# Two of the four sums of gate/up weights formed by accumulating transfers, and five whole pairs instead of six

## The chip, the cores and the metric

One core of a Trainium2 chip runs the whole program. The metric is device microseconds of one execution; a kernel's time is the median of its runs. The engines are TensorE (PE in the profile; its weight loads are PEld), VectorE (DVE), ScalarE (ACT), GpSimd (POOL) and SyncE (SP, which only issues transfers here).

## What is computed

A trunk of two decoder layers on 512 tokens of width 1024, in float32. Each layer has two feed-forward blocks (FFN) around a mixer; so there are four FFNs, numbered 0 to 3 here, and two mixers.

```python
def swiglu(x, w_gate, w_up, w_down):
    return (jax.nn.silu(x @ w_gate) * (x @ w_up)) @ w_down

for layer in range(DEPTH):                    # DEPTH = 2, D_FF = 2816
    h = h + 0.5 * swiglu(rms_norm(h, ffn_norm[layer, 0]), ...)
    mixed = mla_gla_mixer(...) if layer % 2 == 0 else nsa_mixer(...)
    h = h + mixed
    h = h + 0.5 * swiglu(rms_norm(h, ffn_norm[layer, 1]), ...)
return rms_norm(h, final_norm)
```

## The kernel before

Activations lie transposed in SBUF (128 channels x 512 tokens, 8 tiles of x). Every float32 operand is split into a high part (a copy to the format float32r on ScalarE, L150) and a low part (the difference, on VectorE, L151), and a product is three matmuls: high by high, low by high, high by low (`mm3`, L145 to L147). Weights come in raw tiles of 512 KB by SP's queue (`raw`, L91), of which there are three, used in turn for all weights; their high and low parts have three buffers too (`whi`, `wlo`; `shi`, `slo` for up weights and for sums).

An FFN has 22 blocks of 128 hidden channels. A block is a **pair**: its gate and its up product. Two forms of a pair exist:

- **Whole** (`whole`, L366): gate and up weights as they are, each 8 x 3 matmuls of 512 columns into a bank `ps_gu`. The first NP = 6 pairs of an FFN are whole. They take x without the normalising factor `rb`, which is known only after the first of them.
- **By seven products** (`gate_up_steps`, L310): the 2 x 2 blocks (gate, up by two halves of the 1024 input channels) and x in 2 x 2 blocks (two halves of channels, two of tokens) are multiplied in the scheme of Strassen and Winograd with seven products instead of eight. Each is 4 x 3 matmuls of 256 columns (`product`) into `ps_a` or `ps_b`. It needs four sums of weight blocks (`gate_up`, L117: VectorE, L130 to L133, into `sa` and `sb`, one buffer each) and seven forms of x (`ffn_forms`, a generator that is advanced by one step after each whole pair). The sums are split as any weight: into `shi`, `slo` and, for one block that is no sum, `uhi`, `ulo`.

The forms of x take the buffers of the x tiles that the whole pairs read (14 in all): three forms fit beside these tiles, the last four come when the last whole pair has read them. They are made in the last step of the generator, after which the first pair by products starts (L417, L418).

Between the pairs stand **units** (`unit`, L390): the down product of a group of four or five blocks for 128 output channels, into `ps_d`, added to x by VectorE (L397). The weights of pair j+1 are asked for at the start of the turn of pair j (L412), ahead of the whole pair j in the program.

The order of each engine's instructions is set when the program is built: a scheduler goes through the instructions by their place in the program as priority, gives out buffers and models the time; each engine then runs its fixed order and waits on semaphores. An instruction whose inputs and buffers are free early can stand far ahead of its place.

Of the kernel before, what the change touches and what calls it, by code (L numbers as in the profile page):

```python
# [12 lines left out]
F32 = mybir.dt.float32  # L13
R = mybir.dt.float32r
I32 = mybir.dt.int32
AF = mybir.ActivationFunctionType
ALU = mybir.AluOpType
PSUM = bass.MemoryType.PSUM

P = 128  # L20
# [6 lines left out]
NEG = -1e30  # L27
TINY = 1e-30
GROUPS = ((0, 4), (4, 9), (9, 14), (14, 18), (18, 22))
NP = 6  # L30
WARM = 11
H = T // 2
AHEAD = 400
# [7 lines left out]
class Core:  # L41
# [55 lines left out]
    def sparts(self):  # L97
        return (self.fw.tile([P, 1024], R, name=n, tag=n, bufs=3) for n in ("shi", "slo"))

    def sum_tile(self, tag):  # L100
        return self.fw.tile([P, 1024], F32, name=tag, tag=tag, bufs=1)

    def open_sums(self):

        self.fws = ExitStack()
        self.fw = self.fws.enter_context(self.pool("sums", side="right"))
# [10 lines left out]
    def gate_up(self, f, j):  # L117


        V, a = self.nc.vector, self.a  # L120
        w = T
        g = self.raw(a["wgu"][f, j, 0], 1024)
        gh, gl = self.wparts()
        self.split(g, gh, gl)
        u = self.raw(a["wgu"][f, j, 1], 1024)
        ah, al = self.sparts()
        bh, bl = self.sparts()
        uh, ul = (self.fw.tile([P, w], R, name=n, tag=n, bufs=1) for n in ("uhi", "ulo"))
        av, bv = (self.sum_tile(n) for n in ("sa", "sb"))
        V.tensor_add(av[:, :w], g[:, :w], u[:, :w])  # L130
        V.tensor_add(av[:, w:], u[:, :w], u[:, w:])
        V.tensor_add(bv[:, :w], av[:, w:], g[:, :w])
        V.tensor_add(bv[:, w:], bv[:, :w], g[:, w:])  # L133
        self.split(av, ah, al)
        self.split(bv, bh, bl)
        self.split(u[:, w:], uh, ul)
        h0, h1 = slice(0, w), slice(w, 2 * w)
        return [
            (gh[:, h0], gl[:, h0]), (gh[:, h1], gl[:, h1]), (ah[:, h0], al[:, h0]), (bh[:, h0], bl[:, h0]),
            (uh, ul), (ah[:, h1], al[:, h1]), (bh[:, h1], bl[:, h1]),  # L140
        ]

    def mm3(self, ps, lh, ll, rh, rl, start, stop, **k):
# [208 lines left out]
    def ffn_body(self, f, gi, hp, meanwhile, fp, out):  # L352
        nc, a = self.nc, self.a
        V, S = nc.vector, nc.scalar
        if out is not None:
            self.form("gap")
        xs, end = self.ffn_input(gi)
        self.rb = None
        hid, todo, w, forms = {}, [], {}, []

        def done(j, gt, ut):
            V.tensor_mul(ut, gt, ut)
            t = hid[j] = hp.tile([P, 2, T], R, name="hid", tag="hid", bufs=HID)
            self.split(ut, t[:, 0], t[:, 1])

        def whole(j):  # L366

            pt = []
            for s in range(2):
                with ExitStack() as st:  # L370
                    if f and 0 < 2 * j + s < 4:
                        for i in end:
                            st.enter_context(self.tc.issue_after(i.ins))
                    wh, wl = self.first or self.wload(a["wgu"][f, j, s], 1024, keep=self.sparts() if s else None)
                self.first = None
                ps = self.ps("ps_gu", "gu")
                for k in range(KC):
                    c = slice(k * P, (k + 1) * P)
                    self.mm3(ps, wh[:, c], wl[:, c], *xs[k], k == 0, k == KC - 1)
                pt.append(ps)  # L380
            if self.rb is None:
                self.rb = self.norm_stats(None if f else self.sumsq(self.x, fast=True))[1]
            ts = [hp.tile([P, T], F32, name=n, tag=n, bufs=2) for n in ("gt", "ut")]
            for s, t in enumerate(ts):
                V.tensor_mul(t, pt[s], self.rb)
                if s == 0:
                    S.activation(t, t, AF.Silu)
            done(j, *ts)

        def unit(g, c):  # L390
            j0, j1 = g
            wh, wl = self.wload(a["wd"][f, c, :, j0 * P : j1 * P], (j1 - j0) * P)
            ps = self.ps("ps_d", "d")
            for j in range(j0, j1):
                m = slice((j - j0) * P, (j - j0 + 1) * P)
                self.mm3(ps, wh[:, m], wl[:, m], hid[j][:, 0], hid[j][:, 1], j == j0, j == j1 - 1)
            V.scalar_tensor_tensor(out=self.x[c], in0=ps, scalar=0.5, in1=self.x[c], op0=ALU.mult, op1=ALU.add)  # L397

        def steps(j):
            return self.gate_up_steps(hp, w.pop(j), forms, lambda gt, ut: done(j, gt, ut))  # L400

        if f == 0:
            ps = self.ps("warm", "st")
            for _ in range(WARM):
                nc.tensor.matmul(ps[:, :P], self.ones, self.ones, start=True, stop=True)
        making = self.ffn_forms(gi, hp, forms)
        cur = None
        for j in range(JC):
            g = next(i for i, (j0, j1) in enumerate(GROUPS) if j0 <= j < j1)
            if j == GROUPS[g][0] and g > 0:  # L410
                todo += [(GROUPS[g - 1], c) for c in range(KC)]
            if NP <= j + 1 < JC:  # L412
                w[j + 1] = self.gate_up(f, j + 1)
            if j < NP:
                whole(j)
                next(making, None)
                if j == NP - 1:  # L417
                    cur = steps(NP)  # L418
                    next(cur)
            else:  # L420
                for n in range(5):
                    next(cur)
                nxt = None
                if j + 1 < JC:
                    nxt = steps(j + 1)
                    next(nxt)
                next(cur, None)
                cur = nxt
            if j == 3 and meanwhile:
                meanwhile(hp)  # L430
            left = GROUPS[g][1] - j
            for _ in range(-(-len(todo) // left)):
                unit(*todo.pop(0))
        if fp:
            self.ffn_end(f, GROUPS[-1][0], hid, fp, out)
            return
        for c in range(KC):
            unit(GROUPS[-1], c)
# [1064 lines left out]
```

## Time and profile before

| | us |
|---|---|
| three runs, median | 2015.86 |
| lowest and highest | 2014.3 and 2016.45 |
| the profiled execution, its own time | 2014.43 |
| span in its trace, first to last instruction | 2012.6 |
| FFN 0 to 3, body (from the end of the start on) | 308.7, 313.0, 306.0, 313.4 |
| mean granted TensorE clock, share of 2.4 GHz | 0.994 |

The page gives busy times by engine, and the chain of work that ended last, followed back from the last instruction. A matmul's time in the trace is from its start to its modelled end; neighbours overlap, so the step from start to start tells the rate, and the duration doesn't. In square brackets behind an instruction stands how long its engine was idle before it, and what ended that.

### The profile page before, as it was taken

The page shows a single profiled execution, that of the slowest core. Times are in us where ns is not written, and L with a number is a line of the kernel's source. Part 1 is how long each engine was busy: PE and PEld are TensorE (multiplying, and loading weights), DVE is VectorE, ACT ScalarE, POOL GpSimd, SP SyncE. Part 2 cuts the span into 40 slices and gives each one's busy share as a digit, 9 for nine tenths or more (in the row PEclk, how much of TensorE's full clock was granted, in tenths as well). Part 3 has the DMA queues.
Part 4 walks back from the last instruction along what each step waited for, and adds up shares of the span by engine and source line. Part 5 has one row for each costly group of instructions (what it writes and reads, how often), then busy time and mean ns, then how long its engine had stood idle before and what let it go on. Part 6 is the DMA issues. An engine that isn't in the chain of part 4 may idle for free.

```text
span 2012.6 us, 31406 instructions
## 1 busy us (share of the span) xinstructions
PE 1967.7 (98%) x11956; PEld 1736.2 (86%) x11956; DVE 1495.5 (74%) x2569; ACT 1020.2 (51%) x1848; POOL 212.0 (11%) x258
## 2 busy tenths in 40 slices
PE   8999999999999999999999999999899999999997
PEld 6899998898778899998789999888687878999997
DVE  7877775678888677776877777677899868777774
ACT  6444443565674444444544444445598754444443
POOL 0000000200340000001000000111365410000002
PEclk9999999999999999999999999999899999999999
DMA  5333332321323232332323233354400033232332
GB/s 175 93 95 100 113 97 67 109 74 43 87 66 116 89 101 90 106 104 86 124 82 102 96 103 99 89 155 135 117 1 1 27 118 96 86 103 96 102 96 68
DMA packets 71191, 186.41 MB, mean 93 GB/s; under 512 B 9856, under 2 KB 13056, under 8 KB 71040
## 3 DMA queue, kind: packets, MB, share of 16 engines
q1 hardware_dynamic: 70608, 183.36, 29.6%
q8 instruction: 94, 1.54, 0.3%
q10 hardware_dynamic: 432, 1.05, 0.2%
q14 instruction: 57, 0.47, 0.1%
HBM read 172.84 MB, written 2.10 MB: 87 GB/s over the span
## 4 chain that ended last, share of the span: by engine, by line
PE 88%; DVE 6%; ACT 2%; issue 1%; DMA 1%; SPq 0%; POOL 0%; DVEq 0%; POOLq 0%; ACTq 0%
PE ps_d L145 8%; PE ps_d L147 8%; PE ps_d L146 8%; PE ps_a L145 6%; PE ps_a L147 6%; PE ps_a L146 6%; PE ps_b L145 5%; PE ps_b L147 5%; PE ps_b L146 5%; PE ps_gu L145 4%; PE ps_gu L147 4%; PE ps_gu L146 4%; PE ps_p L145 3%; PE ps_p L147 3%; PE ps_p L146 3%
## 5 line engine op out<-in xcount | busy, mean ns | idle before, releaser
L150 ACT CAST whi<-raw 128x512 fp32r<-128x512 f32 (+3 forms) x317 | 257.7, 815 | 353.1 <-PE ps_d L146 119.7
L151 DVE TENSOR_TENSOR wlo<-raw,whi 128x512 fp32r<-128x512 f32 (+3 forms) x317 | 304.4, 962 | 92.0 <-ACT whi L150 90.8
L145 PE MATMUL ps_d<-hid,whi 128*128 128x512 f32 x672 | 265.2, 398 | 0.0
L147 PE MATMUL ps_d<-hid,wlo 128*128 128x512 f32 x672 | 264.5, 395 | 0.0
L146 PE MATMUL ps_d<-hid,whi 128*128 128x512 f32 x672 | 263.6, 393 | 0.0
L145 PE MATMUL ps_a<-bh,shi 128*128 128x256 f32 x768 | 217.0, 283 | 0.0
L146 PE MATMUL ps_a<-bl,shi 128*128 128x256 f32 x768 | 216.5, 282 | 0.0
L147 PE MATMUL ps_a<-bh,slo 128*128 128x256 f32 x768 | 216.0, 281 | 0.0
L215 POOL TENSOR_TENSOR ssq<-ssq,sq 128x512 f32<-128x512 f32 x30 | 46.0, 1534 | 1098.4 <-ACT sq L214 1098.4
L147 PEld LDWEIGHTS ps_d<-hid,wlo 128*128 128x128 f32 x672 | 126.1, 188 | 30.4 <-DVE wlo L151 0.7
L145 PEld LDWEIGHTS ps_d<-hid,whi 128*128 128x128 f32 x672 | 126.1, 188 | 25.8 <-ACT whi L150 1.0
L146 PEld LDWEIGHTS ps_d<-hid,whi 128*128 128x128 f32 x672 | 126.2, 188 | 25.0
L146 PEld LDWEIGHTS ps_a<-bl,shi 128*128 128x128 f32 x768 | 144.6, 188 | 1.2
L147 PEld LDWEIGHTS ps_a<-bh,slo 128*128 128x128 f32 x768 | 145.2, 189 | 0.0
L145 PEld LDWEIGHTS ps_a<-bh,shi 128*128 128x128 f32 x768 | 144.1, 188 | 1.2
L130 DVE TENSOR_TENSOR sa<-raw 128x512 f32<-128x512 f32 x64 | 44.2, 690 | 131.7 <-DMA raw<-wgu 131.7
L397 DVE SCALAR_TENSOR_TENSOR x<-ps_d,x 128x512 f32<-128x512 f32 x152 | 104.0, 686 | 42.3 <-PE ps_d L147 42.0
L587 POOL TENSOR_TENSOR pr<-pr,sums 128x128 f32<-128x128 f32 (+3 forms) x160 | 114.1, 746 | 101.3 <-DVE sums L1007 19.8
L150 ACT CAST uhi<-raw 128x512 fp32r<-128x512 f32 x64 | 39.7, 621 | 160.5 <-PE ps_b L146 111.3
L150 ACT CAST shi<-sa 128x1024 fp32r<-128x1024 f32 x64 | 67.3, 1051 | 76.8 <-PE ps_a L146 67.9
L151 DVE TENSOR_TENSOR slo<-sa,shi 128x1024 fp32r<-128x1024 f32 x64 | 78.3, 1223 | 28.5 <-ACT shi L150 28.4
L568 ACT ACTIVATE pr<-sm_s,sm_m 128x512 f32<-128x512 f32 (+3 forms) x160 | 89.7, 564 | 12.1 <-DVE sm_m L564 11.6
(450 smaller groups left out, 5576.9 us busy)
## 6 DMA issues: line engine op xcount, KB each, us to landing
raw<-wgu SPq DMA_DIRECT2D x175, 512.0 KB, 3.8
raw<-wd SPq DMA_DIRECT2D x96, 256.0 KB, 2.7
raw<-wd SPq DMA_DIRECT2D x64, 320.0 KB, 2.9
raw<-wo SPq DMA_DIRECT2D x32, 256.0 KB, 2.8
raw<-w1t SPq DMA_DIRECT2D x16, 512.0 KB, 3.6
raw<-w0v SPq DMA_DIRECT2D x8, 512.0 KB, 3.6
raw<-w0t SPq DMA_DIRECT2D x6, 512.0 KB, 3.8
rt_s<-rt_f SPq DMA_DIRECT2D x48, 64.0 KB, 2.0
```

What stands on the lines that cost most here:

```text
L130: V.tensor_add(av[:, :w], g[:, :w], u[:, :w])
L145: mm(ps, lh, rh, start=start, stop=False, **k)
L146: mm(ps, lh, rl, start=False, stop=False, **k)
L147: mm(ps, ll, rh, start=False, stop=stop, **k)
L150: self.nc.scalar.copy(hi, src)
L151: self.nc.vector.tensor_sub(lo, src, f32v(hi))
L215: (nc.vector if last or fast else nc.gpsimd).tensor_add(acc, acc, sq)
L397: V.scalar_tensor_tensor(out=self.x[c], in0=ps, scalar=0.5, in1=self.x[c], op0=ALU.mult, op1=ALU.add)
L568: nc.scalar.activation(p, s[:, :n], AF.Exp, bias=mn, scale=-1.0, accum_out=sums)
L587: self.nc.gpsimd.tensor_mul(o, o, w[:, qb : qb + 1].to_broadcast([P, n]))
```

## The change

Two sums are no longer made by VectorE. For pair j the program loads the up weights into `sa` (all 1024 columns) and their first half into `sb`; then GpSimd's queue issues two transfers that read weights from HBM and add them to what lies in SBUF: the first half of the gate weights onto `sb`, the second half of the up weights onto the first half of `sa`. VectorE makes the other two sums, into the second half of `sb` and into a new tile `sc`. `sa` and `sb` have two buffers each. Up weights of such a pair no longer pass through a raw tile. The order of the blocks in the seven products follows. NP is 5, so each FFN has five whole pairs and seventeen by products, and the generator of the forms is run to its end after the last whole pair.

```diff
-NP = 6
+NP = 5
...
-    def sum_tile(self, tag):
-        return self.fw.tile([P, 1024], F32, name=tag, tag=tag, bufs=1)
...
-        g = self.raw(a["wgu"][f, j, 0], 1024)
+        g, u = a["wgu"][f, j, 0], a["wgu"][f, j, 1]
+        h0, h1 = slice(0, w), slice(w, 2 * w)
+
+        av = self.fw.tile([P, 1024], F32, name="sa", tag="sa", bufs=2)
+        bv = self.fw.tile([P, 1024], F32, name="sb", tag="sb", bufs=2)
+        cv = self.fw.tile([P, w], F32, name="sc", tag="sc", bufs=1)
+        self.nc.sync.dma_start(out=av, in_=u)
+        self.nc.sync.dma_start(out=bv[:, h0], in_=u[:, h0])
+        self.nc.gpsimd.dma_start(out=bv[:, h0], in_=g[:, h0], accum_op=ALU.add)
+        self.nc.gpsimd.dma_start(out=av[:, h0], in_=u[:, h1], accum_op=ALU.add)
+        g = self.raw(g, 1024)
         gh, gl = self.wparts()
         self.split(g, gh, gl)
-        u = self.raw(a["wgu"][f, j, 1], 1024)
         ah, al = self.sparts()
         bh, bl = self.sparts()
-        uh, ul = (self.fw.tile([P, w], R, name=n, tag=n, bufs=1) for n in ("uhi", "ulo"))
-        av, bv = (self.sum_tile(n) for n in ("sa", "sb"))
-        V.tensor_add(av[:, :w], g[:, :w], u[:, :w])
-        V.tensor_add(av[:, w:], u[:, :w], u[:, w:])
-        V.tensor_add(bv[:, :w], av[:, w:], g[:, :w])
-        V.tensor_add(bv[:, w:], bv[:, :w], g[:, w:])
+        ch, cl = (self.fw.tile([P, w], R, name=n, tag=n, bufs=1) for n in ("uhi", "ulo"))
+        V.tensor_add(bv[:, h1], av[:, h0], g[:, h0])
+        V.tensor_add(cv, bv[:, h1], g[:, h1])
+        self.split(bv, bh, bl)
         self.split(av, ah, al)
-        self.split(bv, bh, bl)
-        self.split(u[:, w:], uh, ul)
-        h0, h1 = slice(0, w), slice(w, 2 * w)
+        self.split(cv, ch, cl)
         return [
-            (gh[:, h0], gl[:, h0]), (gh[:, h1], gl[:, h1]), (ah[:, h0], al[:, h0]), (bh[:, h0], bl[:, h0]),
-            (uh, ul), (ah[:, h1], al[:, h1]), (bh[:, h1], bl[:, h1]),
+            (gh[:, h0], gl[:, h0]), (gh[:, h1], gl[:, h1]), (bh[:, h0], bl[:, h0]), (bh[:, h1], bl[:, h1]),
+            (ah[:, h1], al[:, h1]), (ah[:, h0], al[:, h0]), (ch, cl),
         ]
...
                 if j == NP - 1:
+                    for _ in making:
+                        pass
                     cur = steps(NP)
```

## Rows read from the trace of the kernel before

**Rows 1.** Page, parts 1 and 4: engines: busy us (share) xinstructions; chain

```profile
PE 1967.7 (98%) x11956; PEld 1736.2 (86%) x11956; DVE 1495.5 (74%) x2569; ACT 1020.2 (51%) x1848; POOL 212.0 (11%) x258
...
PE 88%; DVE 6%; ACT 2%; issue 1%; DMA 1%; SPq 0%; POOL 0%; DVEq 0%; POOLq 0%; ACTq 0%
```

**Rows 2.** Windows: stretch, length, busy (x) PE PEld DVE ACT POOL, PEclk, DMA, GB/s

```profile
0.00:36.30 36.30, 30.19 (x129) 22.59 (x129) 24.39 (x43) 24.45 (x33) 0.70 (x6) 1.00 0.66 225
36.30:345.00 308.70, 308.70 (x1970) 279.60 (x1971) 226.25 (x333) 133.90 (x218) 0.00 (x0) 1.00 0.30 93
...
1661.60:1975.00 313.40, 313.40 (x2001) 283.81 (x2000) 230.10 (x334) 137.65 (x222) 0.00 (x0) 1.00 0.31 96
```

**Rows 3.** Timeline of PE: start, us, operation; ends of 22, then of 25

```profile
81.74 0.40 PE L147 MATMUL ps_gu<-xh,wlo 128*128 128x512 f32 x1
...
86.64 0.39 PE L147 MATMUL ps_gu<-xh,wlo 128*128 128x512 f32 x1
...
120.91 0.28 PE L145 MATMUL ps_b<-bh,whi 128*128 128x256 f32 x1
...
123.79 0.28 PE L145 MATMUL ps_a<-bh,whi 128*128 128x256 f32 x1
```

**Rows 4.** Groups by shape: line, operation, count, busy us, mean ns

```profile
L145 PE MATMUL ps_a<-bh,shi 128*128 128x256 f32 x768 | 217.0, 283 | 0.0
...
L145 PE MATMUL ps_gu<-xh,whi 128*128 128x512 f32 x192 | 76.5, 398 | 4.9 <-DVE gt L385 1.8 <-ACT whi L150 1.5 <-DVE x L555 0.9
...
L130 DVE TENSOR_TENSOR sa<-raw 128x512 f32<-128x512 f32 x64 | 44.2, 690 | 131.7 <-DMA raw<-wgu 131.7
```

**Rows 5.** Timeline: last of whole(4) in FFN 0; DVE idle, FFN 0 to 3

```profile
69.72 0.40 PE L147 MATMUL ps_gu<-xh,slo 128*128 128x512 f32 x1
...
81.82 0.69 DVE L385 TENSOR_TENSOR ut<-ps_gu,rb 128x512 f32<-128x512 f32 x1 [3.56 <-PE ps_gu L147]
...
658.60 0.69 DVE L385 TENSOR_TENSOR ut<-ps_gu,rb 128x512 f32<-128x512 f32 x1 [1.79 <-PE ps_gu L147]
...
1012.78 0.69 DVE L385 TENSOR_TENSOR ut<-ps_gu,rb 128x512 f32<-128x512 f32 x1 [0.79 <-PE ps_gu L147]
...
1701.00 0.69 DVE L385 TENSOR_TENSOR ut<-ps_gu,rb 128x512 f32<-128x512 f32 x1 [3.28 <-PE ps_gu L147]
```

**Rows 6.** Timeline of DVE: low part of sum b, two neighbouring pairs

```profile
164.72 1.21 DVE L151 TENSOR_TENSOR slo<-sb,shi 128x1024 fp32r<-128x1024 f32 x1
...
182.58 1.22 DVE L151 TENSOR_TENSOR slo<-sb,shi 128x1024 fp32r<-128x1024 f32 x1
```

**Rows 7.** DMA issues: count, KB, median us to landing

```profile
raw<-wgu SPq DMA_DIRECT2D x175, 512.0 KB, 3.8
raw<-wd SPq DMA_DIRECT2D x96, 256.0 KB, 2.7
...
x<-xT SPq DMA_DIRECT2D x2, 512.0 KB, 7.8
```

**Rows 8.** Instructions of tile cmc: count, ns, first and last start us

```profile
L1293 DVE TENSOR_TENSOR sc_s<-ps_sct,cmc x4: 676/682/692, 1430.7 to 1556.1; 128x512 f32<-128x512 f32 x4
L1255 SPq DMA_DIRECT2D cmc<-cmc x1: 422/422/422, 1312.3 to 1312.3; - x1
```

**Rows 9.** Timeline, FFN 0: up weights of whole(1) made, first read

```profile
17.61 1.21 DVE L151 TENSOR_TENSOR slo<-raw,shi 128x1024 fp32r<-128x1024 f32 x1
...
21.71 0.39 PE L145 MATMUL ps_gu<-xh,shi 128*128 128x512 f32 x1
```

**Rows 10.** Timeline, FFN 1: last POOL add of the statistics, their use

```profile
598.98 1.32 POOL L215 TENSOR_TENSOR ssq<-ssq,sq 128x512 f32<-128x512 f32 x1 [0.95 <-ACT sq L214]
...
612.32 0.95 PE L178 MATMUL ps_s<-inv_dm,ssq 128*128 128x1 f32 x8
```

**Rows 11.** One DVE shape, 520 to 600 us, then 100 to 345 us

```profile
L151 DVE TENSOR_TENSOR wlo<-raw,whi 128x512 fp32r<-128x512 f32 x13 | 11.3, 879 | 0.6 <-ACT whi L150 0.6
...
L151 DVE TENSOR_TENSOR wlo<-raw,whi 128x512 fp32r<-128x512 f32 x13 | 8.9, 684 | 2.3 <-ACT whi L150 2.2
```

## The prediction

> **What bounds the kernel now.** Read the page first, its part 1 and the shares of the chain that ended last: TensorE is busy 98% of the span and makes 88% of the chain; VectorE is busy 74% and makes 6% [rows 1]. So an edit that takes work off VectorE alone has nothing to win by itself. Then the busy time by stretch, with cuts where a feed-forward block (FFN) leaves its start: from 36.30 to 345.00 us PE is busy 308.70 of 308.70 us, and in the last FFN 313.40 of 313.40, while VectorE is idle for 82 and 83 us of these [rows 2]. "Busy" there is modelled with overlap, so the third view is the timeline of PE. Its starts are evenly spaced: 22 matmuls of 512 columns from 81.74 to 86.64 us are 21 steps of 0.233 us, and 25 of 256 columns from 120.91 to 123.79 are 24 steps of 0.120 us [rows 3]. There is no gap to close in the body of an FFN; its time is the number of matmuls by their step. Only fewer columns on PE can make it shorter.
>
> **Part 1: one whole pair less in each FFN.** A whole pair is 2 x 8 x 3 = 48 matmuls of 512 columns (six pairs in four FFNs are 1152, six groups of 192 like the one shown); a pair by seven products is 7 x 4 x 3 = 84 of 256 columns (64 pairs are 5376; the group shown has 768 of them) [rows 4]. By the steps of [rows 3]: 48 x 0.2333 = 11.20 us against 84 x 0.120 = 10.08 us. The saving is 1.12 us an FFN, 4 x 1.12 = **4.5 us**, and all of it lies on the path, because PE is dense on both sides. By columns alone one would expect an eighth; the narrow matmul has the worse step, and so it is a tenth.
>
> **Part 2: two adds leave VectorE.** Before, 64 pairs have four adds of 0.69 us [rows 4]; after, 68 pairs have two. That is 256 - 136 = 120 adds, 83 us of VectorE work. It counts as nothing: the engine idles 27% of the body and PE waits for none of it [rows 2]. What it does buy is room at the hand-over, below.
>
> **Part 3: what is added to the transfers.** A pair loaded 2 x 512 KB on SP's queue; now SP loads 512 + 256 + 512 KB and GpSimd's queue adds two of 256 KB: 768 KB more, for 68 pairs 53 MB on the page's 186. The DMA share of 0.30 in the body [rows 2] goes to about 0.4, and no engine comes near its limit. Cover: PE's dense stream; if it is gone, the cost is in the rivals.
>
> No transfer of the trace is issued by GpSimd, nor does one accumulate, so its price has only bounds. Below: a plain load of 256 KB, 2.7 us; above: the slowest landing, 512 KB beside the loads of the start, 7.8 us [rows 7]. I take 5 us, about twice the plain load, since the destination is read too. The chain of a sum is then 3.8 us (the load) plus 5, at most 3.8 + 7.8 = 11.6 us. Room in the body: the splits of sum b lie 17.9 us apart in neighbouring pairs [rows 6], and with two buffers a sum may load from the split of the pair before last, so 35.7 us stand against 11.6. **Zero on the path**, even at the upper bound.
>
> **Part 4: what stands in queues.** SP now waits for sum buffers too, and behind such a wait stand the down-weight loads; they have three raw buffers to themselves for all but one load of a pair, where two were taken before, so they gain cover. GpSimd's queue was empty in the body [rows 2]. At the start of FFN 1 to 3 it holds the adds of the statistics; an accumulating transfer that waits ahead of them for its plain load holds them up to 3.8 us. The last such add ends at 600.3 and its sum is read by PE at 612.32 [rows 10]: 12 us of cover, cost zero.
>
> **Part 5: the hand-over.** The seven forms of x are needed 11.2 us earlier. The last four need buffers that the x tiles of the last whole pair hold, so they move with it. FFN 0 is the tight one. The last whole pair then ends at 69.95 us, where whole(4) ends now; VectorE, without a gap until then, is first idle at 81.82 - 3.56 = 78.26 [rows 5]. Of that backlog the two weight splits of whole(5) (2 x 1.2) and two adds (1.4) go; four low parts of forms (4 x 1.2) come: 78.3 - 3.8 + 4.8 = 79.3 us. PE has beside it two down units (24 x 0.233 = 5.6 us) and three products (36 x 0.120 = 4.3 us): 69.95 + 5.6 + 4.3 = 79.9 before it needs the fourth form. It fits by half a microsecond, and the table work for rope in that backlog can yield. In FFN 1, 2 and 3 VectorE's first idle time ends with the very last matmul of whole(4) (658.60, 1012.78, 1701.00), so it has no backlog there [rows 5]. Cost taken: zero, up to 3 us in FFN 0.
>
> **The sum.** The profiled execution took 2014.43 us, 1.8 us around its span of 2012.6. 2014.43 - 4.5 = 2009.9; the median of the three runs, 2015.86, is 1.4 us above it, so the forecast for the median is **2011.4 us**. A measurement of this kernel tells about 0.2%, 4 us, from no change; the forecast lies just beyond that line.
>
> **Rival 1: the early loads collide (no change).** Loads are issued as soon as their memory is free: cmc goes out at 1312.3 us and is first read at 1430.7 [rows 8]. The sums of the first two pairs have free buffers when an FFN opens, so their 1.5 MB go out among the first loads. In FFN 0 these move 225 GB/s [rows 2]; 0.8 to 1.6 MB are 3.5 to 7.0 us for the load queued behind. The up weights of whole(1) are ready at 18.82 and read at 21.71 [rows 9], 2.9 us of margin: 0.6 to 4.1 us lost in FFN 0, so 2012.0 to 2015.5, middle 2013.8. Against it: the loads of x, which the start really waits for, are issued earlier still.
>
> **Rival 2: GpSimd is kept from issuing (slower).** In the trace GpSimd and VectorE do disturb each other: the same 128x512 difference of two SBUF tiles takes 879 ns where GpSimd works and 684 where it is idle [rows 11]. If the accumulating transfers of the first pair wait until VectorE pauses, in FFN 0 they go at 78.3, land at 81.0 to 86.1, and are split (2.3 us) by 83.3 to 88.4; the third product needs them at 69.95 + 5.6 + 2 x 1.44 = 78.4. PE loses 4.9 to 10.0 us, 2011.8 to 2016.9; with the same loss in a second FFN 2016.7 to 2026.9. It decides for slower from 8.5 us of waiting on. Against it: these transfers can go before 36 us, when VectorE is busy 24.39 of 36.30 us [rows 2], and in FFN 1 to 3 VectorE pauses before the hand-over [rows 5].
>
> The Trainium skill ("SBUF — State Buffer", sections "SBUF: two separate sides" and "Who interferes with whom") states this rule against the change: a transfer issued by GpSimd has its descriptors written into SBUF by that engine, and it is locked out while VectorE runs an operation in a two-port mode; an operation with two SBUF inputs disturbs only GpSimd's reads. By that, the sums and splits here would not stop it, only the few table operations of FFN 0 could, and the sum would stay at 2011.4; [rows 11] agrees for operations with two SBUF inputs, and the lock no row here shows.
>
> **Rival 3: the sums come late in every pair.** It needs a chain of more than 35.7 us, three times the upper bound; then each microsecond costs 68, and the time would be 2080 or more. Or a plain accounting miss: the hand-over of FFN 0 stalls 3 us, 2014.4, which is no change.
>
> **How the numbers follow.** Forecast 0.56, its own range 2009.0 to 2013.0: at best 2 us of shifted order in the stretches between FFNs, at worst 1.5 us of stall. Rival 1 or the stall of FFN 0: 0.27. Rival 2: 0.14. Rival 3: 0.03. Faster by over 0.2% (below 2011.8): 0.7 of the forecast and a little of rival 1, 0.42. Within 0.2%: the rest of these and the low end of rival 2, 0.16 + 0.24 + 0.04, so 0.44. Slower: 0.14. The range, 2009.0 to 2018.0, takes in rival 1 and the low half of rival 2.
>
> **What would show it.** Right: PE's groups with ps_gu fall to 160 of each kind, PE stays without a gap from 36 us to the end of each FFN, starts still 0.233 and 0.120 us apart, the two sums' adds gone, all mixers as long as now. Rival 1: PE gaps before 36 us that end with a weight split, behind loads of the sums. Rival 2: accumulating transfers of FFN 0 that start only near 78 us, and a gap before the third product. Wrong altogether if a wider step of the matmuls or a gap at each sum's first use shows up.

## The result, and the profile after

The changed kernel takes **2032.0 us** (median of four runs, 2031.0 to 2035.0) against 2016.15 us of the kernel before beside it: a ratio of 1.0087, 95% interval 1.0074 to 1.0100 (the two medians alone give 1.0079). It is 16 us slower where 4.5 us faster was forecast. Its profiled execution took 2032.79 us with a span of 2031.0; the span before was 2012.6, so 18.4 us between these two profiles are to be found.

Page of the kernel after: engines (part 1), the two large DMA queues (part 3) and the issues of the weights (part 6: count, KB, median us to landing).

```profile
PE 1971.4 (97%) x12100; PEld 1745.1 (86%) x12100; DVE 1427.5 (70%) x2461; ACT 1029.7 (51%) x1872; POOL 329.2 (16%) x394
...
q1 hardware_dynamic: 80400, 201.19, 31.6%
q0 software_dynamic: 19584, 35.66, 10.9%
...
raw<-wgu SPq DMA_DIRECT2D x107, 512.0 KB, 3.7
sa<-wgu SPq DMA_DIRECT2D x68, 512.0 KB, 4.2
raw<-wd SPq DMA_DIRECT2D x96, 256.0 KB, 2.7
...
sb<-wgu SPq DMA_DIRECT2D x68, 256.0 KB, 3.2
sa<-wgu POOLq DMA_DIRECT2D x68, 256.0 KB, 3.8
sb<-wgu POOLq DMA_DIRECT2D x68, 256.0 KB, 4.7
```

Against [rows 1], VectorE has lost 68 us of work and GpSimd has gained 117, its 136 issues at 0.88 us. None of that is on the path. What is on it stands in the waits of PE and VectorE (engine, what waited, for what: us in total, times, longest us). The first three lines are PE's, the last is VectorE's.

```profile
PE ps_b L147 <- DVE gt L335: 6.3, 3, 4.1
...
PE ps_gu L147 <- DVE x L559: 5.1, 1, 5.1
PE ps_gu L147 <- DVE gt L387: 3.8, 3, 2.8
```

```profile
DVE sb L135 <- DMA sa<-wgu: 51.2, 16, 6.8
```

L135 is the add that makes the second half of sum b from sum a and the gate weights. Sixteen times it stood at the head of VectorE's queue and waited for the accumulating transfer into sum a (by the landings it was 21 times of 68; the view puts five of these waits down to something else). L335 is the addition that frees a PSUM half for PE; it stands behind L135. PE has four gaps of 1.0 to 4.1 us in the bodies between the pairs, which end at 722.15, 1060.82, 1092.92 and 1786.65 us, and each comes 1.1 to 2.2 us behind the end of such a wait.

The longest of these waits, in FFN 3, first on the queues and VectorE, then on PE (timeline: start, us, engine, operation, and in brackets the idle time before it and what ended it):

```profile
1772.14 1.22 DVE L153 TENSOR_TENSOR slo<-sa,shi 128x1024 fp32r<-128x1024 f32 x1
...
1773.39 0.33 SPq L125 DMA_DIRECT2D sa<-wgu  x1
...
1778.77 0.86 POOL L128 DMA_DIRECT2D sa<-wgu  x1 [1.34 <-DVE wlo L153]
...
1782.25 0.28 PE L147 MATMUL ps_a<-bh,whi 128*128 128x256 f32 x1
...
1785.57 0.69 DVE L135 TENSOR_TENSOR sb<-sa,raw 128x512 f32<-128x512 f32 x1 [6.80 <-DMA sa<-wgu]
1786.18 0.42 DVE L335 TENSOR_TENSOR gt<-ps_b,sa 128x256 f32<-128x256 f32 x1
...
1786.65 0.58 PE L147 MATMUL ps_b<-bh,shi 128*128 128x256 f32 x1 [4.13 <-DVE gt L335]
1787.04 0.41 PE L148 MATMUL ps_b<-bl,shi 128*128 128x256 f32 x1
1787.25 0.41 PE L149 MATMUL ps_b<-bh,slo 128*128 128x256 f32 x1
```

Read it as one chain. VectorE finishes the split of the sum a of two pairs earlier at 1773.36, and SP loads the free buffer at 1773.39. That load landed at 1778.11, GpSimd issued the accumulating transfer at 1778.77, and it landed at 1785.49: 12.1 us in all. VectorE had come to the add at 1778.77 (1785.57 less 6.80). PE then ran out of PSUM and stood from 1782.5 to 1786.65. Behind the gap its starts are 0.21 us apart, not 0.120 as in [rows 3].

The windows say why (columns as in [rows 2]; the first two lie around the start of FFN 1, the third behind this stop):

```profile
580.00:603.00 23.00, 17.90 (x77) 14.11 (x76) 17.85 (x23) 12.49 (x22) 11.08 (x10) 0.96 0.84 240
603.00:607.50 4.50, 4.50 (x11) 3.53 (x12) 3.62 (x4) 3.98 (x5) 0.38 (x1) 0.50 0.13 33
1787.00:1792.00 5.00, 5.00 (x20) 4.52 (x20) 3.47 (x6) 2.15 (x5) 0.00 (x0) 0.50 0.43 134
```

After PE stood still for 4.1 or 5.1 us the granted clock was 0.50, the 1.2 GHz level, for some 5 us: 11 matmuls of 512 columns in 4.5 us, where 0.233 us a step gives 19. That is 1.9 us more behind the one stop, and 2.6 behind the other (20 of 256 columns in 5 us, where 0.120 us a step gives 41). The body of FFN 3 as a whole, where the last line of [rows 2] had no gap:

```profile
1714.00:1994.00 280.00, 275.87 (x1870) 255.62 (x1869) 175.85 (x253) 120.64 (x204) 24.38 (x28) 0.99 0.50 132
```

**Where the 18.4 us are.** In the table, "lost" is the sum over PE's neighbouring starts of their distance less the undisturbed step (0.233 us for 512 columns, 0.178 for 384, 0.120 for 256, 0.065 for others); steps at the low clock count in it. "Opening" runs from an FFN's first ps_gu matmul to its last, "body" from there to the last down matmul, each summed over the four FFNs. "PE work" is the rest of the FFNs, "between" all that lies outside them. Each line adds up to the span of that profile. The ratio is that of the timed runs, with its interval.

| kernel | PE work | openings lost | bodies lost | between | span | ratio to before |
|---|---|---|---|---|---|---|
| before | 1410.2 | 11.0 | 3.5 | 587.9 | 2012.6 | |
| after | 1405.8 | 18.1 | 15.6 | 591.6 | 2031.0 | 1.0087 (1.0074 to 1.0100) |
| e1_five | 1405.8 | 23.5 | 3.5 | 587.3 | 2020.1 | 1.0036 (1.0023 to 1.0048) |
| e2_six | 1410.2 | 18.5 | 11.8 | 589.3 | 2029.7 | 1.0089 (1.0075 to 1.0103) |
| e3_loads_only | 1405.8 | 15.8 | 4.0 | 588.2 | 2013.8 | 1.0021 (1.0012 to 1.0030) |
| e4_other_add | 1405.8 | 21.0 | 15.2 | 590.8 | 2032.8 | 1.0080 (1.0066 to 1.0093) |
| e5_three | 1405.8 | 14.6 | 4.0 | 589.4 | 2013.8 | 1.0008 (0.9999 to 1.0017) |
| e6_plain | 1405.8 | 14.4 | 4.9 | 588.2 | 2013.2 | 1.0020 (1.0010 to 1.0030) |
| e7_hold | 1405.8 | 29.2 | 18.6 | 586.9 | 2040.4 | 1.0128 (1.0112 to 1.0144) |
| e9_late_add | 1405.8 | 18.5 | 4.0 | 590.3 | 2018.6 | 1.0034 (1.0021 to 1.0046) |
| e12_three_behind | 1405.8 | 14.1 | 4.0 | 584.9 | 2008.7 | 0.9996 (0.9987 to 1.0005) |
| e13_five_behind | 1405.8 | 10.7 | 4.2 | 584.2 | 2004.9 | 0.9976 (0.9968 to 0.9985) |
| e14_six_three | 1410.2 | 11.2 | 5.0 | 588.6 | 2015.0 | 1.0026 (1.0015 to 1.0036) |

From before to after: PE work -4.4, openings +7.1, bodies +12.1, between +3.7. A profile is one execution and lies up to 4.2 us from the median of its kernel (e3_loads_only, whose profile is its fastest run), so the table is for the split and the ratios are for the size. The medians that the text does not name are, in us: e3_loads_only 2019.8, e4_other_add 2032.0, e5_three 2016.8, e6_plain 2018.2, e9_late_add 2022.3, e14_six_three 2018.8, with the kernel before beside them at 2013.6 to 2015.2.

### The profile page after: what moved, and what is told of

It reads as the page before. It is cut to its first block, busy times and chain, and to the rows that moved or that the text cites. A ratio compares the mean times of both kernels' runs of the same rounds, so it can differ in the third digit from the quotient of the medians.

```text
span 2031.0 us, 32319 instructions
## 1 busy us (share of the span) xinstructions
PE 1971.4 (97%) x12100; PEld 1745.1 (86%) x12100; DVE 1427.5 (70%) x2461; ACT 1029.7 (51%) x1872; POOL 329.2 (16%) x394
## 3 DMA queue, kind: packets, MB, share of 16 engines
q0 software_dynamic: 19584, 35.66, 10.9%
## 5 line engine op out<-in xcount | busy, mean ns | idle before, releaser
L152 ACT CAST shi<-sb 128x1024 fp32r<-128x1024 f32 x68 | 71.5, 1051 | 195.8 <-PE ps_a L148 191.0
L147 PE MATMUL ps_b<-bh,shi 128*128 128x256 f32 x544 | 154.7, 284 | 6.3 <-DVE gt L335 6.3
L148 PE MATMUL ps_b<-bl,shi 128*128 128x256 f32 x544 | 153.9, 283 | 0.0
L147 PE MATMUL ps_a<-bh,shi 128*128 128x256 f32 x544 | 153.8, 283 | 0.0
L149 PE MATMUL ps_b<-bh,slo 128*128 128x256 f32 x544 | 153.4, 282 | 0.0
L148 PE MATMUL ps_a<-bl,shi 128*128 128x256 f32 x544 | 153.4, 282 | 0.0
L149 PE MATMUL ps_a<-bh,slo 128*128 128x256 f32 x544 | 152.9, 281 | 0.0
L147 PEld LDWEIGHTS ps_b<-bh,shi 128*128 128x128 f32 x544 | 102.5, 188 | 10.0 <-DVE gt L335 7.2
L148 PEld LDWEIGHTS ps_b<-bl,shi 128*128 128x128 f32 x544 | 103.0, 189 | 2.4
L149 PEld LDWEIGHTS ps_b<-bh,slo 128*128 128x128 f32 x544 | 103.5, 190 | 0.0
```

Source lines behind the costliest of these rows:

```text
L147: mm(ps, lh, rh, start=start, stop=False, **k)
L148: mm(ps, lh, rl, start=False, stop=False, **k)
L149: mm(ps, ll, rh, start=False, stop=stop, **k)
L152: self.nc.scalar.copy(hi, src)
```

## The experiments

Two theories stand beside each other. **The add waits:** the accumulating transfer lands after VectorE has come to L135, and what PE needs is queued behind it; this is the bodies' loss. **The openings are crowded:** the first pairs' loads and VectorE work come where an FFN opens. The rivals to both are that the sixth whole pair was needed, or that the DMA traffic itself slows PE.

**One part alone.** e1_five is the kernel before with five pairs; e2_six is the changed kernel with six.

```diff
-NP = 6
+NP = 5
...
                 if j == NP - 1:
+                    for _ in making:
+                        pass
                     cur = steps(NP)
```

> The kernel before with five whole pairs an FFN instead of six; all four sums still made by VectorE. If the loss lies in the accumulated sums, this keeps only the gain of part 1: 4.5 us less PE time, about 2011.5 us, PE without a gap in the body. If the fifth whole pair was needed as cover (the hand-over with four sums on VectorE comes 11 us earlier), a gap of some microseconds at the hand-over of FFN 0 and a time of 2014 to 2020; if the loss of the change lies in the number of pairs, 2025 to 2032.

```diff
-NP = 5
+NP = 6
```

> The changed kernel with six whole pairs, so the sums by accumulating transfers alone. If the loss lies in the sums: 2032 plus the 4.5 us of part 1, about 2036 us (2030 to 2040, since the stalls depend on the order of the work). If the loss lies in the fifth pair: about 2016, as before.

Both are slower than before: 2021.9 and 2033.3 us. The sums by transfer lose 8.3 us in the bodies and 7.5 in the openings even with six pairs; five pairs lose nothing in the bodies but 12.5 us in the openings, with no accumulating transfer in the kernel. So neither part does alone what was forecast, and e1_five lies between the ranges that were expected of it. The timeline of e1_five at the opening of FFN 0, VectorE and then PE, shows the second mechanism:

```profile
30.78 0.69 DVE L130 TENSOR_TENSOR sa<-raw 128x512 f32<-128x512 f32 x1 [2.62 <-DMA raw<-wgu]
31.39 0.69 DVE L131 TENSOR_TENSOR sa<-raw 128x512 f32<-128x512 f32 x1
...
33.73 0.16 DVE L197 TENSOR_SCALAR rs_v<-ps_s 128x4 f32<-128x4 f32 x1
33.80 0.68 DVE L132 TENSOR_TENSOR sb<-sa,raw 128x512 f32<-128x512 f32 x1
34.40 0.17 DVE L199 RECIPROCAL rc<-rs_q 128x4 f32<-128x4 f32 x1
34.52 0.69 DVE L133 TENSOR_TENSOR sb<-sb,raw 128x512 f32<-128x512 f32 x1
...
35.99 0.87 DVE L182 TENSOR_SCALAR dg<-ident,rc 128x128 f32<-128x128 f32 x4
...
37.01 2.05 PE L184 MATMUL ps_b<-dg,ones 128*128 128x512 f32 x2 [3.83 <-DVE dg L182]
```

The four adds of the first seven-product pair stand in VectorE's queue ahead of, and between, the steps of the rms factor (rs_v, rc, dg). They wait 2.62 us for their weights; the factor comes late, and PE waits 3.83 us for it. The same step (dg) in the kernel before, 3.6 us earlier:

```profile
32.35 0.88 DVE L182 TENSOR_SCALAR dg<-ident,rc 128x128 f32<-128x128 f32 x4
```

**The accumulation taken out.** e3_loads_only leaves the two GpSimd transfers away; e4_other_add gives L135 other inputs.

```diff
-        self.nc.gpsimd.dma_start(out=bv[:, h0], in_=g[:, h0], accum_op=ALU.add)
-        self.nc.gpsimd.dma_start(out=av[:, h0], in_=u[:, h1], accum_op=ALU.add)
```

> The changed kernel without the two accumulating transfers of a pair; their plain loads stay, so the two sums hold only the up weights. If VectorE's add that reads sum a waits for the accumulating transfer and holds up its queue: the gaps at 720, 1059, 1091 and 1782 us vanish, some 11 us with the slow steps behind the last, 2018 to 2022 us. If only the early loads at the openings of the FFNs cost time: these stay, 2028 to 2032. If both and the accumulating transfers also fill the openings: down to 2012.

```diff
-        V.tensor_add(bv[:, h1], av[:, h0], g[:, h0])
+        V.tensor_add(bv[:, h1], bv[:, h0], av[:, h1])
```

> The changed kernel with the add of VectorE that makes the second half of sum b taking the first half of sum b plus the second half of the up weights, so that it waits for the accumulating transfer that lands first (sum b), by 3 to 5 us earlier, instead of that of sum a. If the wait of this add at the head of VectorE's queue makes the gaps in the body: most of their 11 us go, 2021 to 2026 us. If the time is lost to the openings or to the DMA traffic itself: 2030 to 2033.

Without the accumulation the bodies fall from 15.6 to 4.0 us: the gaps are those of the transfers into the sums, not of the extra bytes of the plain loads. e4_other_add gained nothing, against the expectation. Its wait on VectorE:

```profile
DVE sb L135 <- DMA sb<-wgu: 96.0, 50, 7.2
```

With the earlier input the add also stands earlier in VectorE's queue (VectorE comes to it 4.2 us after the release of its pair's buffer of sum a, median, against 12.8 in the changed kernel), and it waits more often, not less (50 times against 16). Here, where the order of a queue is written when the kernel is built, a nearer input gave no slack, because the place of the instruction moved with it.

**Room, place, price.** e5_three gives sum a a third buffer. e9_late_add leaves the transfers and moves the adds. e6_plain keeps queues and bytes and drops the addition.

```diff
-        av = self.fw.tile([P, 1024], F32, name="sa", tag="sa", bufs=2)
+        av = self.fw.tile([P, 1024], F32, name="sa", tag="sa", bufs=3)
```

> The changed kernel with three buffers for sum a instead of two. If the loads of a sum come late because they wait for the split of sum a two pairs before, they now go out a pair (15 us) earlier, the accumulating transfer has landed long before VectorE's add reads it, and the 12 us of gaps in the bodies go: about 2020 us. If the add's place in VectorE's queue follows the load (the order of the queues is fixed when the kernel is built, from modelled times), the add moves up with it and waits as before: 2028 to 2034.

```diff
+        with ExitStack() as st:
+            if j > NP:
+                st.enter_context(self.tc.issue_after(self.low.ins))
-        V.tensor_add(bv[:, h1], av[:, h0], g[:, h0])
-        V.tensor_add(cv, bv[:, h1], g[:, h1])
+            V.tensor_add(bv[:, h1], av[:, h0], g[:, h0])
+            V.tensor_add(cv, bv[:, h1], g[:, h1])
...
-        self.split(av, ah, al)
+        self.low = self.split(av, ah, al)
```

> The changed kernel with VectorE's two adds of a pair queued behind the low part of sum a of the pair before, some 10 us later in its queue; nothing else. If these adds stand too early in the queue and hold up what PE waits for: the 12 us of gaps in the bodies go, 2019 to 2022 us. If the sums are late for their splits as well, the gaps only move to those: 2028 to 2034.

```diff
-        self.nc.gpsimd.dma_start(out=bv[:, h0], in_=g[:, h0], accum_op=ALU.add)
-        self.nc.gpsimd.dma_start(out=av[:, h0], in_=u[:, h1], accum_op=ALU.add)
+        self.nc.gpsimd.dma_start(out=bv[:, h0], in_=g[:, h0])
+        self.nc.gpsimd.dma_start(out=av[:, h0], in_=u[:, h1])
```

> The changed kernel with the two GpSimd transfers of a pair as plain ones, that overwrite instead of adding, so the two sums hold only one of their terms; bytes and queues stay. If the accumulation itself is dear: these land 2.7 to 3.5 us after their issue instead of 3.8 to 4.7, and the gaps in the bodies shrink to a few microseconds, 2020 to 2026 us. If the issue by GpSimd is what makes them slow: landing as in the changed kernel, 2030 to 2034.

The longest kind of wait of L135 in e5_three, and in e9_late_add (there L138, by its added lines):

```profile
DVE sb L135 <- DMA raw<-wgu: 45.5, 26, 5.0
```

```profile
DVE sb L138 <- DMA raw<-wgu: 2.2, 3, 1.0
```

The windows over the body of FFN 3, e5_three and then e9_late_add:

```profile
1703.00:1975.00 272.00, 272.00 (x1858) 252.12 (x1857) 176.87 (x253) 121.15 (x205) 23.52 (x27) 1.00 0.51 133
```

```profile
1709.00:1980.00 271.00, 271.00 (x1853) 251.31 (x1853) 174.96 (x252) 120.23 (x204) 24.38 (x28) 1.00 0.52 137
```

Either cure takes the bodies to 4.0 us, and PE has no gap left there (272.00 of 272.00 us, 271.00 of 271.00). In e5_three the add now waits for the plain load of the gate weights, not for a sum, and nothing of it reaches PE. The accumulating transfers still take 4.0 and 4.8 us in e5_three, as in the changed kernel; a pair's more room, or a later place, hides them. From the release of the buffer to VectorE's coming to the add it is 15.4 us or more in e5_three and 12.3 or more in e9_late_add, against 4.9 to 9.1 us in the 21 late sums of the changed kernel, and no sum is late in either. The DMA share is 0.51 and 0.52, no less than the 0.50 of the changed kernel's window, so the traffic itself does not slow PE in the bodies. e9_late_add stays slower than before for its openings, 18.5 us. That settles the first theory: not the length of the transfer made the gaps, but the distance between the release of its buffer and the place of its first reader in VectorE's queue.

What the addition itself costs is read from e6_plain, queue and landings:

```profile
q0 software_dynamic: 10880, 35.66, 5.3%
...
sa<-wgu POOLq DMA_DIRECT2D x68, 256.0 KB, 2.9
sb<-wgu POOLq DMA_DIRECT2D x68, 256.0 KB, 3.6
```

The addition costs 0.9 and 1.1 us of the 3.8 and 4.7, and twice the time on the DMA engines for the same bytes. With 1 us less, L135 waits 19.9 us for sum a, not 51.2, and the bodies lose 4.9: the changed kernel sat just beyond the edge.

**The openings.** e7_hold queues all that makes the first two seven-product pairs (SP, ScalarE, VectorE) behind the up weights of the whole pair that is traced before each (the fourth and the fifth). In e12_three_behind (with three buffers, FFN 1 to 3) and e13_five_behind (five pairs with VectorE's own sums) the VectorE work goes behind the first use of the rms factor, and the loads behind those of the second and of the fourth whole pair.

```diff
+                with ExitStack() as st:
+                    if j <= NP:
+                        for i in self.held:
+                            st.enter_context(self.tc.issue_after(i.ins))
+                    w[j + 1] = self.gate_up(f, j + 1)
-                w[j + 1] = self.gate_up(f, j + 1)
```

In e7_hold `self.held` is the load and the two halves of the split of a whole pair's up weights; in the other two the condition is `f and j <= NP + 1` (e12_three_behind) and `j + 1 == NP` (e13_five_behind), and it is the following, with 3 for 1 in e13_five_behind:

```diff
-                V.tensor_mul(t, pt[s], self.rb)
+                mul = V.tensor_mul(t, pt[s], self.rb)
+                if j == 0:
+                    self.held = [mul]
...
+            if j == 1:
+                self.held.append(load)
```

> The changed kernel with all that makes the first two seven-product pairs of an FFN (loads, splits, adds) queued behind the weights of the fourth whole pair on SP, ScalarE and VectorE. If the early sums crowd the openings of the FFNs: the 7 us that PE loses there more than before go, 2024 to 2027 us, with the gaps in the bodies as they are. If the openings are slow for another reason: 2030 to 2034.

> The kernel with three buffers for sum a, and in FFN 1 to 3 the loads of the first three seven-product pairs queued behind the up weights of the second whole pair, their VectorE work behind the first use of the rms factor. If the early loads of the sums delay the last attention output weights and the first weights of the FFN: the opening of FFN 1 loses its 3.4 us of idle time and slow steps, 2011 to 2014 us. If the openings lose their time otherwise: 2016 to 2018 as with three buffers alone.

> Five whole pairs with all four sums on VectorE, and the first seven-product pair's loads queued behind the up weights of the fourth whole pair, its VectorE work behind the first use of the rms factor. If in the run with five pairs alone the sums of this pair stood ahead of the rms factor in VectorE's queue and so cost the 12.5 us at the openings: these go, 2011 to 2014 us. If the missing pair was needed as cover for the hand-over: the gaps move to the hand-over, 2017 to 2022.

e14_six_three has `NP = 6` and the three buffers, without any of this.

> The accumulated sums with three buffers for sum a and six whole pairs: beside the run with three buffers and five pairs it prices the pair alone. If a pair by seven products is 1.12 us cheaper in each FFN on PE and all else is equal: 4.5 us above that run, about 2021 us. If five pairs cost as much at the openings as they save: the same time, 2016 to 2018.

e7_hold is the worst of all, 2042 us. The place behind the split was the wrong one (FFN 0, VectorE, then PE):

```profile
32.94 0.18 DVE L200 RECIPROCAL rc<-rs_q 128x4 f32<-128x4 f32 x1 [0.29 <-ACT rs_q L199]
35.70 0.69 DVE L135 TENSOR_TENSOR sb<-sa,raw 128x512 f32<-128x512 f32 x1 [2.58 <-DMA sa<-wgu]
36.31 0.15 DVE L201 TENSOR_TENSOR rs_q<-rc 128x4 f32<-128x4 f32 x1
...
38.72 2.05 PE L185 MATMUL ps_b<-dg,ones 128*128 128x512 f32 x2 [4.91 <-DVE dg L183]
```

The later loads put L135 into the middle of the rms steps, where it waits for its sum, and PE with it. It is the first theory once more, at the opening.

e13_five_behind, with the pair's work behind the factor, is **faster than before: 2009.4 against 2013.6 us, ratio 0.9976 (0.9968 to 0.9985)**. The openings fall from e1_five's 23.5 us to 10.7, below those of before, and the work of a pair less is left (that the same place gives nothing with six pairs was not run, nor the loads' place and VectorE's each alone). VectorE and PE at the same opening:

```profile
32.48 0.88 DVE L182 TENSOR_SCALAR dg<-ident,rc 128x128 f32<-128x128 f32 x4
35.26 0.69 DVE L387 TENSOR_TENSOR gt<-ps_gu,rb 128x512 f32<-128x512 f32 x1 [1.90 <-ACT rb L167]
...
38.79 0.68 DVE L130 TENSOR_TENSOR sa<-raw 128x512 f32<-128x512 f32 x1
...
33.51 1.10 PE L184 MATMUL ps_b<-dg,ones 128*128 128x512 f32 x2 [0.28 <-DVE dg L182]
```

In its profile, the fastest of its eleven runs, 4.4 of 7.7 us are PE work and 3.7 lie between the FFNs, where nothing was changed; the paragraph on the mixers below comes back to these.

e12_three_behind reaches 2012.1 us, no different from before. At the end of the first mixer the loads of the attention's output weights had taken 6.2 to 7.2 us to land in the changed kernel (2.7 to 4.4 before), beside the sums' loads that went out at 579.7 to 581.8 us. In e12_three_behind they take 2.3 to 2.8, and PE goes into FFN 1 with a stop of 1.3 us, as before (3.6 in e5_three, 5.5 in the changed kernel). The gain on e5_three lies in the first mixer (235.1 to 230.0 us, 2.3 of it this stop) and not in the openings as counted in the table, where FFN 2 lost what FFN 1 won. e3_loads_only, without the accumulating transfers, has this stop too (5.2 us), so it comes with the plain loads on SP's queue. The window of e12_three_behind ahead of FFN 1's first matmul at 594.25 us, and the one behind:

```profile
575.00:594.20 19.20, 18.38 (x79) 14.46 (x77) 16.83 (x24) 13.24 (x22) 9.39 (x6) 1.00 0.52 180
594.20:599.00 4.80, 4.75 (x21) 3.87 (x22) 3.85 (x5) 4.03 (x5) 1.76 (x2) 1.00 1.01 327
```

e14_six_three (three buffers and six pairs) is 0.26% above before, where e5_three with five is 0.08% above. The intervals overlap; the difference, 0.18% or 3.6 us, is near the 4.4 us of PE work, though by the profiles five pairs give 3.4 us of it back at the openings. And e12_three_behind with its transfers is no faster than e13_five_behind with four sums on VectorE (0.9996 and 0.9976): no run shows a gain by the transfers, even with their waits cured. The two are not alike in all else, since their openings are ordered differently and lose 14.1 and 10.7 us.

## Why the prediction was wrong, by its own steps

**What bounds the kernel, and part 2: right.** PE is the bound, and 68 us less on VectorE bought nothing (the adds alone fell by 82 us, 83 forecast; the four more pairs by products bring work of their own). But "PE waits for none of it" held for VectorE's work, not for its queue.

**Part 1: right in size, wrong in "all of it lies on the path".** The saving is 4.4 us of PE work (1410.2 to 1405.8), 4.5 forecast. Alone, with the first pair's work put behind the rms factor, the kernel is 4.8 us faster (0.24%; 4.2 by the medians). As it stands it pulls that work into the opening: e1_five lost 12.5 us there.

**Part 3: the step that failed.** The price was good: 4.2 us for the load, 0.66 to the issue, 3.8 to land are 8.7 us against 8.8 forecast. That is partly luck: the load took 0.4 us more than forecast, the 0.66 was not counted, and the transfer took 1.2 less. The longest chain, 12.2 us in a body and 16.3 at the opening of FFN 0, lies above the bound of 11.6. The room was not: "with two buffers a sum may load from the split of the pair before last, so 35.7 us stand against 11.6". The load does go out then, at 1773.39; but the sum's first reader is not its split. It is the add L135, which VectorE reaches at 1778.77: **5.4 us of room**. In the 21 sums that came late it was 4.9 to 9.1 us, against a chain of 7.8 to 12.2. The sum was taken from split to split [rows 6], and the add that stands between was not asked for. The sign was there: [rows 4] has 131.7 us of idle time before the 64 adds L130, ended by the landing of raw, 2 us a pair. These adds already stood where VectorE waits for a transfer. It cost nothing as long as that transfer was a plain load; a load and an accumulation in its place are 5 us later, and what PE needs stood behind. That is a gap at a sum's first use, which the prediction itself named as the sign of being wrong altogether. The DMA share came out at 0.50 in the body, not about 0.4, since the addition takes twice the engines' time; no stop of PE came of that.

**Part 4: half right.** The down-weight loads did not hurt PE. GpSimd's queue did not either. SP's queue did, at a place that the step did not name: the end of the first mixer, where the sums' loads stand with those of the attention's output weights.

**Part 5: right where it looked.** No gap shows at the hand-over of FFN 0 in the changed kernel, and one of 0.46 us ahead of 82.63 us in e13_five_behind, within the "zero, up to 3 us". It looked at the end of the last whole pair only; the cost lay at the opening. Of the 7.1 us that the openings of the changed kernel lose more, 1.9 are the slow steps behind the stop before FFN 1. Three buffers take away 3.5, and e12_three_behind still loses 3.1 more than before; what makes these is open.

**Rival 1: right mechanism, wrong FFN and size.** The early loads did collide, in FFN 1: PE waited 5.1 us for the last x of the mixer, and then ran 4.5 us at the low clock. In FFN 0 the opening lost 8.7 us, 6.4 before; its one long wait is for gt L387 (2.8), which stood behind a split of the sums in VectorE's queue. e5_three, with the same early loads, lost 6.2 us there.

**Rival 2: did not happen.** Its times also count the 4.5 us of part 1 twice: 4.9 to 10.0 us on top of 2011.4 are 2016.3 to 2021.4, and 2021.2 to 2031.4 with a second FFN, not 2011.8 to 2016.9 and 2016.7 to 2026.9. So the measured 2032.0, just above, would not have told against this rival by itself; the places of the transfers do. The first accumulating transfers left GpSimd at 15.7 to 21.9 us, not near 78. The Trainium skill's rule ("SBUF — State Buffer", sections "SBUF: two separate sides" and "Who interferes with whom") says that an operation of VectorE with two SBUF inputs keeps GpSimd from reads of SBUF only, so that it would not hold up these issues. The trace agrees: the 17 issues that lay wholly under such operations took 0.865 us (median), the 29 beside an idle VectorE 0.866, and the longest of all 1.22.

**Rival 3: right in kind, wrong in its condition.** The sums came late, but a chain of 35.7 us was not needed for it; one longer than 5.4 was enough. It was not every pair, 21 of 68, and a wait of VectorE reached PE only where it outlasted PE's own lead (at 1785.57 us, 6.80 of waiting became 4.13 on PE). So it cost 12.1 us in the bodies, not 68 for each microsecond of lateness.

**The mixers** were to stay as long as they were: "between" moved by 3.7 us. In kernels whose code there is the same, the stretch from FFN 0 to FFN 1 took 229.7 to 236.4 us, from FFN 2 to FFN 3 333.2 to 337.8. One part is the stop before FFN 1 (5.5 us from PE's last mixer matmul to its first in the FFN, where before had 1.3). Another is the clock: near the start of the first mixer, the profile of the kernel before (234.8 us for the stretch) ran at 1.2 GHz where e13_five_behind (229.7) ran at full speed. Their windows:

```profile
376.00:382.80 6.80, 6.80 (x34) 6.80 (x34) 2.80 (x11) 1.18 (x2) 0.00 (x0) 0.50 0.26 80
```

```profile
374.00:380.80 6.80, 6.80 (x54) 6.32 (x54) 3.26 (x12) 1.62 (x3) 0.00 (x0) 1.00 0.22 77
```

The 20 matmuls more, of 256 columns, are 2.4 us by the step of 0.120. In the 6 us ahead PE waited 2.0 us in the one and 0.3 in the other; e14_six_three, with six pairs too, waited 1.9 us at the same place and kept a granted clock of 1.00. So the waits seem to go with the sixth pair, which no run was made to show, and the 2.4 us with that one execution: the "between" of before is no undisturbed measure. e1_five, with the longest stretch from FFN 2 to FFN 3, likewise ran at 0.50 from 1350.2 to 1357.0 us. The rest is not explained.

## What to carry to other kernels

When a source of data gets slower, look for its first reader in program order on an in-order engine, not for the last use; the room is from the release of its buffer to that reader's place, and idle time that a DMA already ends before that instruction says that a later landing will be waited for. Whether that wait costs anything is then a question of what stands behind it. When work moves to an earlier stage, ask for every queue what stands behind it there: at an opening that was the rms factor. Another buffer was worth more here (1.0087 to 1.0008) than the saving in the work itself (4.5 us, 0.2%).

## What the runs showed of the hardware

An accumulating transfer of 256 KB from GpSimd took 3.8 to 4.7 us to land (medians), the plain one 2.9 to 3.6, and the addition doubled the DMA engines' time for 35.66 MB from 5.3 to 10.9% of the span. The Trainium skill ("DMA: Bandwidth & Descriptors", section "Anatomy of one DMA — SWDGE (gpsimd) path") gives about 2.0 us plus the bytes at 436 GB/s, an estimate of 2.6 us for 256 KB; the plain transfers here, beside a kernel's other loads, took 0.3 to 1.0 us more, and the measurement decides. From the landing of the plain load to GpSimd's issue behind it lay 0.66 us, and the issue kept GpSimd for 0.87 us.

After two stops of PE, of 5.1 and 4.1 us, the granted clock was 0.50 for some 5 us, and the steps behind them cost 1.9 and 2.6 us more than at full clock. These rows do not tell which stops do this: in the profile of the kernel before the clock was 0.50 from 376.0 to 382.8 us behind three waits of PE of 0.4, 0.7 and 1.0 us, and it stayed at 1.00 in e14_six_three behind three of 0.4, 0.7 and 0.8.
